# Traced durations in the order generator, and a convolution that reads its products from PSUM

## The chip, the cores and the metric

The kernel runs on one core of one Trainium2 chip. A core has five engines that each run their own queue of instructions strictly in order: TensorE (PE, matrix multiplies, with its weight loads shown as PEld), VectorE (DVE), ScalarE (ACT), GpSimd (POOL) and SyncE (SP, which here only issues DMA transfers). They wait for each other through semaphores. Matrix products land in PSUM, an accumulator memory that the kernel uses as eight banks of 128 x 512 float32; everything else on the chip lies in SBUF. The metric is the device time of one execution in microseconds; lower is better.

## The reference, cut to what matters

Two layers over 2048 frames of width 1024, float32. Each layer normalises the frames, scales and shifts them by a conditioning vector, mixes along time, and adds the result back.

```python
def causal_dwconv(x, w):                       # w has 4 taps per channel
    xp = jnp.pad(x, ((0, 0), (k - 1, 0), (0, 0)))
    out = xp[:, 0:s] * w[0]
    for j in range(1, k):
        out = out + xp[:, j:j + s] * w[j]

def rglru_block(h, in_w, conv_w, conv_b, gate_w, gate_b, lam, out_w):       # layer 1
    proj = h @ in_w                            # 1024 -> 2048
    xb, zg = proj[..., :D_RNN], proj[..., D_RNN:]
    xb = causal_dwconv(xb, conv_w) + conv_b
    pre = einsum(xb, gate_w) + gate_b          # 8 blocks of 128, two gates
    r_t, i_t = sigmoid(pre)
    log_a = -8 * r_t * softplus(-lam)
    h_t = exp(log_a) * h_{t-1} + sqrt(1 - exp(2 log_a)) * (i_t * xb)
    return (h * silu(zg)) @ out_w
```

Layer 2 is a gated DeltaNet: a projection 1024 -> 4 x 1024 (q, k, v, z) plus 16 columns, the same 4-tap convolution on q, k and v, a chunked delta rule over 8 heads of 128 channels, a gated norm and an output projection. A last norm ends it.

## The kernel before

**Precision.** Products are made of float32 data split in a high and a low half, so each product of two 1024-deep operands is 8 x 3 matmuls of 128 x 128 weights against 512 columns (`products`, L661 to L668): 24 matmuls, called a job here.

**The order.** Nothing is scheduled at run time. `Weave` (L64 to L135) is a small simulation that runs while the program is built. Every piece of the computation is a Python generator (a thread) that yields what it needs next: an engine with a duration in us (`yield "dve", STT`), a slot of a buffer ring, an event, or a DMA. `run` always lets the thread go next that can start earliest by these durations, and on equal times the one with the lower priority number. The instructions are emitted in that order, so the durations written in the generators decide the order in each engine's queue. They decide nothing else: on the chip an instruction starts when its queue reaches it and its semaphores are met. A third value in a `yield` replaces the default lag (0.2 to 0.3 us) after which a result counts as seen by another engine. The names for the common durations stand at L241: `STT`, `EV`, `CP`, `TR`, `MM`, `M4` for a tap, a VectorE pass over 512 columns, a ScalarE copy, a transpose, a product matmul and a small matmul of 128 columns.

**Layer 1** (two halves of 1024 frames, each in two groups of 512; profile time to about 516 us). For each of 8 channel blocks there is an x panel and a z panel of weights; each makes two jobs, one for each group of frames. `project_thread` runs the jobs one after another at priority 9, so that its products fill whatever TensorE time the other threads leave. A job takes a slot of the PSUM ring `mm` (two banks), for x and for z alike. The other rings of PSUM are `tp`, `c` and `d`, two banks each; `d` is used in layer 1 only for transposes at the start.

- An x job goes to `conv1_thread`: `extend` has POOL copy the last four frames of the group before (L721 or L725), ACT copy the product from PSUM to the SBUF tile `xe` (L727), after which the bank is free, and POOL save the new last four frames (L730). Then POOL makes the first tap with the bias (`xf`, L741), and DVE adds the other three taps one by one in `taps` (L715), each reading `xe` and `xf` and writing `xf`.
- A z job goes to `z1_thread`: ACT makes a tanh from PSUM (L750), DVE combines it with the product in PSUM (L752), after which the bank is free.
- `gates_thread` splits `xf` in halves (`xh` by ACT, L765; `xl` by DVE, L768), runs two times three gate matmuls (`pg`, L774), two tanh, an exp and a square root on ACT, six passes of DVE with the scan over time (L805), two passes of POOL (L792, L812), and stores the result.

Beside this the weights of each panel are split (ACT L643, POOL L649), the second half of the frames is normalised, transposed and split, and the conditioning of layer 2 is computed (L412 on DVE).

**Out1** (about 516 to 696 us) is the output projection of layer 1: 32 jobs.

**Layer 2** (about 696 to 1784 us): 128 jobs, a convolution with `extend`, POOL L958 and the same `taps`, and for each of 8 heads and 16 blocks of 128 frames the delta rule. `recurrence_thread` is a chain of short steps: two products with the state (`pp`, L1369), `zt` on DVE (L1378), `py` on PE (L1386), `yt` on ACT (L1392), `pS` on PE (L1398), the new state on DVE (L1411). The jobs of the projection are put between these steps by the generator. **Out2** (from about 1784 us): 16 blocks of 128 frames.

Of the kernel before, what the change touches and what calls it, by code (L numbers as in the profile page):

```python
# [8 lines left out]
F32 = mybir.dt.float32  # L9
F32R = mybir.dt.float32r  # L10
# [55 lines left out]
class Weave:  # L66
# [8 lines left out]
    LAG = {"pe": 0.2, "act": 0.3, "dve": 0.3, "pool": 0.2}  # L75

    def __init__(self):
        self.free = dict.fromkeys(("pe", "act", "dve", "pool", "sp", "dma"), 0.0)
        self.threads = []
        self.now = 0.0  # L80
# [19 lines left out]
    def start(self, th):  # L100
# [8 lines left out]
        return max(th.t, self.free.get(w[0], 0.0))  # L109

    def run(self):
        while self.threads:
# [26 lines left out]
def trunk_kernel(ctx, tc, x, c, ada_w, ada_b, ada_c, norm_c, final_g, w1, cw1, cb1, gate_w, gate_b, lam, ow1,  # L139
# [21 lines left out]
    def flat(ap):  # L161
# [13 lines left out]

    middle = cp.tile([P, P], F32, name="middle")
    pool.tensor_copy(out=middle, in_=upper)
    pool.tensor_scalar(middle[0:64, :], middle[0:64, :], -1.0, 0.0, ALU.add, ALU.add)
# [15 lines left out]
    carry1 = cp.tile([P, KT, 4], F32, name="carry1")  # L194
# [6 lines left out]
            "ss": ("xp", 4), "rs": ("xp", 4)}  # L201
    tags |= {f"tf{n}": ("l1", 1) for n in range(6)}
    tags |= {t: ("ps", 2) for t in ("mm", "tp", "c", "d")}
    tags |= {t: ("l1", n) for t, n in {"xe1": 2, "xf1": 2, "tg": 4, "th": 2, "tz": 2, "gw": 1, "gh": 1, "gl": 1, "ada": 1, "ng": 1}.items()}
    tags |= {"yf": ("o1", 1), "yh": ("o1", 2), "yl": ("o1", 2), "xr": ("o1", 2), "g1": ("o1", 1)}
    tags |= {t: ("l2", n) for t, n in {
        "xe": 2, "xf": 2, "kt": KTN, "qt": QTN, "vt": 1, "ec": 3, "gr": 1, "ac": 4, "atn": 4, "kd": 4, "vn": 4,
# [4 lines left out]
    for t in ("xe", "xf", "vt", "ec", "gr", "ab", "gin", "gg", "spe", "spd"):  # L212
        tags[t] = ("l2a", tags[t][1])
# [27 lines left out]
    STT, EV, CP, TR, MM, M4 = 0.665, 0.605, 0.48, 0.109, 0.2163, 0.218  # L241
# [203 lines left out]
    def scale_thread(xt, done):  # L445
# [12 lines left out]
        yield "dve", STT  # L458
# [97 lines left out]
    def split_thread(layer, pt, release_, hh, hl, k, done, tag):  # L556
# [3 lines left out]
        yield "act", 0.665  # L560
# [7 lines left out]
        else:  # L568
            yield "dve", 0.33
# [4 lines left out]
        else:  # L574
            yield "dve", EV
# [35 lines left out]
    def panels_thread():  # L611
        yield ev("adaissue", 2)
        ahead = []
        for name, panels, _ in plans:
            for m, p in enumerate(panels):
# [31 lines left out]
                else:  # L647
                    yield "pool", 2.3
# [21 lines left out]
    def job(name, jobs, n):  # L670
# [8 lines left out]
        mtok = yield slots["mm"]  # L679
        pt = ps.tile([P, TC], F32, tag="mm", name="mm")  # L680
# [4 lines left out]
        if layer == 1:  # L685
            w.spawn((conv1_thread if kind == "x" else z1_thread)(u, m, i, pt, mtok), 2, 0.2)
# [30 lines left out]
    def extend(xe, pt, mtok, carry, key, g):  # L717
# [4 lines left out]
        else:  # L722
            yield ev("carry", key, g - 1)
            yield "pool", 0.14
# [4 lines left out]
        yield "pool", 0.14, 0.0  # L729
# [3 lines left out]
    def conv1_thread(u, n, i, pt, mtok):  # L733
        etok = yield slots["xe1"]
        xe = tile_([P, TC + 4], "xe1", "xe1")
# [1007 lines left out]
```

## Time and profile before

| what | value |
|---|---|
| median of 3 runs | 1986.4 us (1982.22 to 1989.81) |
| the profiled execution's own time | 1980.38 us |
| its span, first to last instruction | 1978.6 us |
| mean granted TensorE clock | 0.985 |
| busy: PE, DVE, ACT, POOL | 93%, 75%, 53%, 37% |
| HBM traffic over the span | 162 GB/s |

The span is what the trace resolves; the own time has 1.8 us around it. "Busy" counts the time in which at least one instruction of an engine runs. The matmuls of TensorE overlap each other, so a matmul row shows about 400 ns while matmuls start about 227 ns apart.

### The profile page before, as it was taken

The page shows a single profiled execution, that of the slowest core. Times are in us where ns is not written, and L with a number is a line of the kernel's source. Part 1 is how long each engine was busy: PE and PEld are TensorE (multiplying, and loading weights), DVE is VectorE, ACT ScalarE, POOL GpSimd, SP SyncE. Part 2 cuts the span into 40 slices and gives each one's busy share as a digit, 9 for nine tenths or more (in the row PEclk, how much of TensorE's full clock was granted, in tenths as well). Part 3 has the DMA queues.
Part 4 walks back from the last instruction along what each step waited for, and adds up shares of the span by engine and source line. Part 5 has one row for each costly group of instructions (what it writes and reads, how often), then busy time and mean ns, then how long its engine had stood idle before and what let it go on. Part 6 is the DMA issues. An engine that isn't in the chain of part 4 may idle for free.

```text
span 1978.6 us, 31398 instructions
## 1 busy us (share of the span) xinstructions
PE 1846.2 (93%) x10286; PEld 1500.3 (76%) x10286; DVE 1475.7 (75%) x3171; ACT 1046.7 (53%) x2555; POOL 724.1 (37%) x1215
## 2 busy tenths in 40 slices
PE   6998889999998998898989999999999999999998
PEld 3776667787787777777777778777888888878887
DVE  6788798887644567778977898567778778877654
ACT  3655567666411236465555555555656566654321
POOL 4555664444200135345344544333333334311101
PEclk9999999999999999999999999999999999999999
DMA  8355655654578724547764457455465555577751
GB/s 334 103 157 158 223 168 169 200 178 153 175 198 210 225 74 140 145 114 176 189 161 130 119 125 191 128 147 147 119 152 147 131 133 140 149 219 221 225 186 64
DMA packets 511724, 322.77 MB, mean 163 GB/s; under 512 B 371268, under 2 KB 439236, under 8 KB 511560
## 3 DMA queue, kind: packets, MB, share of 16 engines
q1 hardware_dynamic: 511560, 320.77, 57.4%
q8 instruction: 81, 1.33, 0.3%
q14 instruction: 83, 0.68, 0.1%
HBM read 219.93 MB, written 100.73 MB: 162 GB/s over the span
## 4 chain that ended last, share of the span: by engine, by line
PE 46%; DVE 21%; DMA 10%; issue 6%; ACT 6%; POOL 5%; SPq 5%; DVEq 0%; POOLq 0%; ACTq 0%
PE mm L667 21%; PE mmo L667 12%; DVE xf L715 6%; DMA raw<-in_w 2%; DVE ttmp L1249 2%; DVE tblk L1252 2%; PE pg L774 1%; DMA xt<-x_d 1%; SPq L1187 1%; SPq L512 1%; DVE acc L412 1%; PE pp L1369 1%; PE pS L1398 1%; PE pkk L1129 1%; PE pS L1399 1%
## 5 line engine op out<-in xcount | busy, mean ns | idle before, releaser
L715 DVE SCALAR_TENSOR_TENSOR xf<-xe,cw_s,xf 128x512 f32<-128x512 f32 x384 | 331.4, 866 | 46.7 <-POOL xf L958 24.1
L649 POOL TENSOR_TENSOR wlo<-raw,whi 128x1024 fp32r<-128x1024 f32 x48 | 120.6, 2512 | 99.7 <-ACT whi L643 81.2
L1249 DVE TENSOR_TENSOR ttmp<-blk,tblk 128x60 f32<-128x60 f32 (+24 forms) x496 | 118.3, 238 | 24.9 <-DMA blk<-blk_d 11.5
L643 ACT CAST whi<-raw 128x1024 fp32r<-128x1024 f32 x96 | 100.4, 1045 | 64.5 <-DMA raw<-in_w 54.7
L1252 DVE TENSOR_TENSOR tblk<-tblk,ttmp 128x60 f32<-128x60 f32 (+24 forms) x496 | 122.3, 247 | 10.0 <-POOL tblk L1243 0.2
L730 POOL COPY carry<-xe 128x4 f32<-128x4 f32 x128 | 40.3, 315 | 239.2 <-ACT xe L727 237.1
L727 ACT COPY xe<-mm 128x512 f32<-128x512 f32 x128 | 73.9, 578 | 74.0 <-PE mm L667 73.0
L667 PE MATMUL mm<-hh_('in2', 0)_5201,whi 128*128 128x512 f32 x256 | 105.0, 410 | 4.1 <-ACT xe L727 4.1
L667 PE MATMUL mmo<-oh,yh 128*128 128x512 f32 x256 | 101.1, 395 | 7.8 <-DVE xr L922 7.2
L667 PE MATMUL mm<-hh_('in2', 1)_12203,whi 128*128 128x512 f32 x256 | 105.2, 411 | 2.8 <-ACT xe L727 2.8
L667 PE MATMUL mm<-hh_('in2', 0)_5424,whi 128*128 128x512 f32 x256 | 103.7, 405 | 2.1 <-ACT xe L727 1.5
L667 PE MATMUL mm<-hh_('in2', 0)_5201,wlo 128*128 128x512 f32 x256 | 105.3, 411 | 0.0
L667 PE MATMUL mm<-hl_('in2', 0)_5425,whi 128*128 128x512 f32 x256 | 104.9, 410 | 0.0
L667 PE MATMUL mm<-hl_('in2', 0)_5202,whi 128*128 128x512 f32 x256 | 104.6, 409 | 0.0
L667 PE MATMUL mm<-hh_('in2', 1)_12379,wlo 128*128 128x512 f32 x256 | 104.4, 408 | 0.0
L667 PE MATMUL mm<-hh_('in2', 1)_12203,wlo 128*128 128x512 f32 x256 | 104.4, 408 | 0.0
L667 PE MATMUL mm<-hh_('in2', 0)_5424,wlo 128*128 128x512 f32 x256 | 104.0, 406 | 0.0
L667 PE MATMUL mm<-hl_('in2', 1)_12204,whi 128*128 128x512 f32 x256 | 103.8, 405 | 0.0
L667 PE MATMUL mm<-hl_('in2', 1)_12380,whi 128*128 128x512 f32 x256 | 103.2, 403 | 0.0
L667 PE MATMUL mm<-hh_('in2', 1)_12379,whi 128*128 128x512 f32 x256 | 103.1, 403 | 0.0
L667 PE MATMUL mmo<-oh,oh 128*128 128x512 f32 (+1 forms) x264 | 102.0, 386 | 0.2 <-DVE tz L986 0.2
L667 PE MATMUL mmo<-ol,oh 128*128 128x512 f32 (+1 forms) x264 | 102.1, 387 | 0.0
(324 smaller groups left out, 5698.7 us busy)
## 6 DMA issues: line engine op xcount, KB each, us to landing
raw<-in_w SPq DMA_DIRECT2D x96, 512.0 KB, 4.2
araw<-in_ada_w SPq DMA_DIRECT2D x32, 512.0 KB, 4.4
xt<-x_d SPq DMA_DIRECT2D x32, 512.0 KB, 4.5
xt_d<-xb SPq DMA_DIRECT2D x192, 64.0 KB, 2.6
xk<-xt_d SPq DMA_DIRECT2D x24, 512.0 KB, 5.5
xt<-in_x SPq DMA_DIRECT2D x16, 512.0 KB, 4.9
ada<-in_ada_w SPq DMA_DIRECT2D x16, 512.0 KB, 9.1
y_d<-tz SPq DMA_DIRECT2D x32, 256.0 KB, 3.1
```

The source lines that it names most:

```text
L412: dve.scalar_tensor_tensor(acc, raw[:, k, :], ck, acc, ALU.mult, ALU.add)
L512: sp.dma_start(out=dst[c_], in_=tb[32 * c_:32 * c_ + 32])
L643: act.copy(hi, raw)
L649: pool.tensor_tensor(lo, raw, f(hi), ALU.subtract)
L667: pe.matmul(pt, lhsT=lhs[a][:, k, :], rhs=rhs[b][:, k, :], start=(k == 0 and n == 0), stop=(k == KT - 1 and n == 2))
L715: dve.scalar_tensor_tensor(xf, xe[:, 1 + j:1 + j + TC], wc[:, j:j + 1], xf, ALU.mult, ALU.add)
L727: act.copy(xe[:, 4:4 + TC], pt)
L730: pool.tensor_copy(out=carry, in_=xe[:, TC:TC + 4])
L774: pe.matmul(pg, lhsT=a[:, g, :], rhs=b, start=(q == 0), stop=(q == 2))
L1129: pe.matmul(pkk[:, b, :], lhsT=kc, rhs=kc, start=True, stop=True)
L1249: dve.tensor_tensor(tmp, blk[:, j, j + 1:32].unsqueeze(2).to_broadcast([P, r, c_]), t[:, j, 0:c_].unsqueeze(1).to_broadcast([P, r, c_]), A ...
L1252: dve.tensor_tensor(t[:, j + 1:32, 0:c_], t[:, j + 1:32, 0:c_], tmp, ALU.subtract)
```

## The change

Three things change together.

1. **The durations.** The names at L241 and some thirty further durations of the generators are replaced by others. `STT` 0.665 to 0.78, `EV` 0.605 to 0.61, `CP` 0.48 to 0.49, `TR` 0.109 to 0.112, `MM` 0.2163 to 0.2275, `M4` 0.218 to 0.23. Other examples: the weight split on POOL 2.3 to 2.45, the scan 0.665 to 1.41, POOL's last pass of the gates 1.23 to 1.42, its four-column copies 0.14 to 0.27, the passes of the gates on DVE 0.605 to between 0.69 and 0.85, scaling a block of `ec` 0.14 to 0.27, the four groups of tiny matmuls of `levels_thread` 0.38, 0.88, 0.4 and 0.9 to 1.1, 1.1, 1.0 and 1.1. `Weave` also gets a kind of matmul `mm` for the 512-column products, which costs 0.087 more when the matmul before it was a small one.
2. **The convolution of layer 1 reads PSUM.** The copy to `xe` and POOL's three instructions for an x job go. ACT makes the last tap with the bias from PSUM into `xf`, columns 3 to 511, and copies the first three and last three columns of the product to a small tile `edge1`. DVE adds the other three taps, reading the product in PSUM and `xf` in SBUF, and the bank is then free. The first three columns of `xf` come from `edge1` by a multiply, a reduction and an addition of the bias, on tiny shapes.
3. **Four banks.** z jobs of layer 1 take a bank of the ring `d`, x jobs stay on `mm`.

Besides, `xh` gets a ring of its own (it shared one with `xe`), and the constant `middle` is made when layer 2 begins instead of at the start. What is computed stays the same. The core of the diff:

```diff
+    SWITCH = 0.087
+    ENGINE = {"mm": "pe"}
...
-                self.free[w[0]] = t + w[1]
-                th.t = t + w[1] + (w[2] if len(w) > 2 else self.LAG[w[0]])
+                dur = w[1]
+                if w[0] in ("pe", "mm"):
+
+                    if w[0] == "mm" and self.small:
+                        dur += self.SWITCH
+                    self.small = w[0] == "pe"
+                e = self.ENGINE.get(w[0], w[0])
+                self.free[e] = t + dur
+                th.t = t + dur + (w[2] if len(w) > 2 else self.LAG[e])
...
-    STT, EV, CP, TR, MM, M4 = 0.665, 0.605, 0.48, 0.109, 0.2163, 0.218
+    STT, EV, CP, TR, MM, M4 = 0.78, 0.61, 0.49, 0.112, 0.2275, 0.23
...
-                yield "pe", dur, 0.0
+                yield "mm", dur, 0.0
...
-        mtok = yield slots["mm"]
-        pt = ps.tile([P, TC], F32, tag="mm", name="mm")
+
+        bank = "d" if layer == 1 and kind == "z" else "mm"
+        mtok = yield slots[bank]
+        pt = ps.tile([P, TC], F32, tag=bank, name="mm")
...
+    def convolve(xf, pt, mtok, wc, bias, edge, key, g, bank):
+
+
+        yield "act", 0.66 if bias is not None else 0.57, 0.0
+        if bias is None:
+            act.activation(xf[:, 3:TC], pt[:, 3:TC], AF.Copy, scale=wc[:, 3:4])
+        else:
+            act.activation(xf[:, 3:TC], pt[:, 3:TC], AF.Identity, bias=bias, scale=wc[:, 3:4])
+        yield "act", 0.18, 0.1
+
+        if g < S // TC - 1:
+            act.copy(edge[:, 6 * g + 3:6 * g + 9].rearrange("p (a b) -> p a b", b=3), window(pt[:, 0:3], (TC - 3, 2), (1, 3)))
+        else:
+            act.copy(edge[:, 6 * g + 3:6 * g + 6], pt[:, 0:3])
+        w.set(ev("edge", key, g))
+        for j in range(3):
+            yield "dve", STT, 0.13 if j < 2 else 0.05
+            dve.scalar_tensor_tensor(xf[:, 3:TC], pt[:, j:j + TC - 3], wc[:, j:j + 1], xf[:, 3:TC], ALU.mult, ALU.add)
+        put(bank, mtok)
+        if g > 0:
+            yield ev("edge", key, g - 1)
+        etok = yield slots["ed"]
+        yield "dve", 0.09, 0.1
+        pr = tile_([P, 3, 4], "ed", "ed")
+        dve.tensor_tensor(pr, window(edge[:, 6 * g:6 * g + 3], (1, 3), (1, 4)), wc.unsqueeze(1).to_broadcast([P, 3, 4]),
+                          ALU.mult)
+        yield "dve", 0.09, 0.1
+        dve.tensor_reduce(out=xf[:, 0:3], in_=pr, axis=mybir.AxisListType.X, op=ALU.add)
+        if bias is not None:
+            yield "dve", 0.14, 0.1
+            dve.tensor_scalar(xf[:, 0:3], xf[:, 0:3], bias, None, ALU.add)
+        put("ed", etok)
...
     def conv1_thread(u, n, i, pt, mtok, bank):
-        etok = yield slots["xe1"]
-        xe = tile_([P, TC + 4], "xe1", "xe1")
         yield ev("columns")
-        yield from extend(xe, pt, mtok, carry1[:, n, :], ("x", n), u * NTC + i)
         ftok = yield slots["xf1"]
-        yield "pool", 0.76
         xf = tile_([P, TC], "xf1", "xf1")
-        pool.tensor_scalar(xf, xe[:, 1:1 + TC], cw1_s[:, n, 0:1], cb1_s[:, n:n + 1], ALU.mult, ALU.add)
-        yield from taps(xe, xf, cw1_s[:, n, :])
-        put("xe1", etok)
+        yield from convolve(xf, pt, mtok, cw1_s[:, n, :], cb1_s[:, n:n + 1], edge1[:, n, :], ("x", n), u * NTC + i, bank)
```

More of the change, by code (lines that the diff above doesn't have):

```diff
@@ L75 @@
     LAG = {"pe": 0.2, "act": 0.3, "dve": 0.3, "pool": 0.2}
+    SWITCH = 0.087
+    ENGINE = {"mm": "pe"}
     def __init__(self):
         self.free = dict.fromkeys(("pe", "act", "dve", "pool", "sp", "dma"), 0.0)
+        self.small = True
         self.threads = []
@@ L210, in trunk_kernel @@
         "gs": 2, "eg": 2}.items()}
-    for t in ("xe", "xf", "vt", "ec", "gr", "ab", "gin", "gg", "spe", "spd"):
+    for t in ("xe", "xf", "vt", "ec", "gr", "middle", "ab", "gin", "gg", "spe", "spd"):
         tags[t] = ("l2a", tags[t][1])
@@ L559, in split_thread @@
         ttok = yield slots[tag]
-        yield "act", 0.665
+        yield "act", 0.71
         h = tile_([P, TC], tag, "h")
@@ L685, in job @@
         if layer == 1:
-            w.spawn((conv1_thread if kind == "x" else z1_thread)(u, m, i, pt, mtok), 2, 0.2)
+            w.spawn((conv1_thread if kind == "x" else z1_thread)(u, m, i, pt, mtok, bank), 2, 0.2)
         elif kind == "z":
@@ L744, in conv1_thread, with z1_thread @@
         w.set(ev("xf", u, n, i), (xf, ftok))
-    def z1_thread(u, n, i, pt, mtok):
+    def z1_thread(u, n, i, pt, mtok, bank):
         ztok = yield slots["tz"]
@@ L752, in z1_thread @@
         dve.scalar_tensor_tensor(tz, tz, 1.0, pt, ALU.add, ALU.mult)
-        put("mm", mtok)
+        put(bank, mtok)
         w.set(ev("tz", u, n, i), (tz, ztok))
@@ L775, in gates_thread @@
             w.spawn(gate_thread(u, n, i, g, pg, ctok), 3)
-        put("xe1", etok)
+        put("xh", etok)
         put("xr", ltok)
@@ L945, in phase1_end_thread @@
         enter("l2", "l2a")
+        middle = tile_([P, P], "middle", "middle")
+        pool.tensor_copy(out=middle, in_=upper)
+        pool.tensor_scalar(middle[0:64, :], middle[0:64, :], -1.0, 0.0, ALU.add, ALU.add)
+        w.set(ev("middle"), middle)
         w.set(ev("l2"))
@@ L1045, in decay_thread @@
         yield "pe", 1.1
+        middle = yield ev("middle")
         pgc = ps.tile([P, 3, NB * NH], F32, tag="tp", name="pgc")
@@ L1449, in outputs_thread @@
         for b in range(TB):
-            yield "act", 0.255, 0.0 if b < TB - 1 else 0.27
+            yield "act", 0.295, 0.0 if b < TB - 1 else 0.27
             act.activation(oo[:, b, :], oo[:, b, :], AF.Copy, scale=ro[:, b:b + 1])
```

81 lines of the change are left out of this document (41 added, 40 removed).

## The prediction

> **What bounds the kernel now.** I read the table of stages first, then the waits of TensorE by stage, then one stall in order of time, then the rows of the instructions that the change touches. The boundaries of the stages are where the kind of work changes; 310 splits layer 1 where the normalising and splitting of its second half has ended.
>
> ```profile
> core 0: us, PE busy (x) PEld busy (x) DVE busy (x) ACT busy (x) POOL busy (x), PEclk, DMA share, GB/s
> 0.00:50.00 50.00, 30.52 (x103) 18.03 (x104) 32.83 (x75) 18.87 (x32) 21.44 (x34) 0.94 0.87 331
> 50.00:310.00 260.00, 228.91 (x945) 179.65 (x945) 219.43 (x259) 158.76 (x223) 154.85 (x151) 0.95 0.52 158
> 310.00:500.00 190.00, 184.47 (x809) 148.77 (x808) 157.67 (x198) 130.84 (x171) 80.12 (x93) 1.00 0.56 180
> 500.00:700.00 200.00, 189.25 (x815) 152.82 (x814) 107.59 (x143) 50.21 (x63) 29.44 (x35) 0.99 0.69 201
> 700.00:1400.00 700.00, 647.89 (x4102) 529.11 (x4100) 546.04 (x1464) 393.51 (x1195) 292.21 (x544) 0.99 0.56 143
> 1400.00:1790.00 390.00, 383.46 (x2649) 319.80 (x2648) 304.70 (x896) 241.25 (x749) 124.56 (x304) 1.00 0.59 153
> 1790.00:1979.00 189.00, 181.67 (x878) 152.11 (x875) 107.48 (x141) 53.30 (x126) 21.51 (x55) 0.99 0.54 166
> ```
>
> TensorE is the bound: 1846 of 1979 us busy, and from 1400 on almost without a hole. What a change can win is its idle time, length minus busy: 19.5, 31.1, 5.5, 10.8, 52.1, 6.5 and 7.3 us. In 50 to 310 it idles 12.0% of the time, in 310 to 500, with the same kind of job, 2.9%; DVE is about as busy in both (84% and 83%), but POOL has 60% in the one and 42% in the other. The granted clock is 0.95 against 1.00 as well, so the early stage loses twice. As all later work of TensorE follows in line, a microsecond won here should come off the end, as long as nothing else is late at the hand-over.
>
> Who ends the idle time, in 50 to 310 and then in 310 to 500:
>
> ```profile
> PE pg L774 <- DVE xl L768: 20.9, 9, 5.2
> PE pg L774 <- ACT xh L765: 1.2, 3, 0.6
> ```
> ```profile
> PE pg L774 <- DVE xl L768: 0.8, 3, 0.3
> ```
>
> So 22.1 of the 31.1 us (71%) are nine to twelve stalls of the gate matmuls, which wait for the halves of `xf`, the convolution's result. One of them, in order of time, by engine (POOL, DVE, PE; start, length):
>
> ```profile
> 122.36 1.27 POOL L812 TENSOR_TENSOR tz<-tz,tg 128x512 f32<-128x512 f32 x1
> 123.59 2.79 POOL L649 TENSOR_TENSOR wlo<-raw,whi 128x1024 fp32r<-128x1024 f32 x1
> ```
> ```profile
> 122.30 1.87 DVE L715 SCALAR_TENSOR_TENSOR xf<-xe,cw_s,xf 128x512 f32<-128x512 f32 x1 [0.51 <-POOL xf L741]
> 124.10 0.70 DVE L506 STREAM_TRANSPOSE xb<-xt 128x512 f32<-128x512 f32 x1
> 124.73 2.21 DVE L715 SCALAR_TENSOR_TENSOR xf<-xe,cw_s,xf 128x512 f32<-128x512 f32 x1
> 126.86 0.68 DVE L768 TENSOR_TENSOR xl<-xf,xh 128x512 fp32r<-128x512 f32 x1
> ```
> ```profile
> 121.94 0.39 PE L667 MATMUL mm<-hl_('in1', 0)_481,whi 128*128 128x512 f32 x1
> 122.17 0.39 PE L667 MATMUL mm<-hh_('in1', 0)_480,wlo 128*128 128x512 f32 x1
> 122.58 0.49 PE L774 MATMUL pg<-xh,gh 128*128 128x512 f32 x1
> 127.59 0.80 PE L774 MATMUL pg<-xl,gh 128*128 128x512 f32 x1 [4.52 <-DVE xl L768]
> 128.19 0.63 PE L774 MATMUL pg<-xh,gl 128*128 128x512 f32 x1
> 128.61 0.63 PE L667 MATMUL mm<-hh_('in1', 0)_480,whi 128*128 128x512 f32 x1
> ```
>
> TensorE stands 4.52 us for `xl`, which is queued on DVE behind two taps that take 1.87 and 2.21 us while POOL runs. After it matmuls start 0.42 us apart instead of 0.23: the clock was lowered, and that is the second loss. Now what a tap costs, and what it could cost from PSUM (shortest, median, longest ns of all; then the means in 50 to 310):
>
> ```profile
> L715 DVE SCALAR_TENSOR_TENSOR xf<-xe,cw_s,xf x384: 702/747/2935, 58.4 to 1737.2; 128x512 f32<-128x512 f32 x192
> ```
> ```profile
> L752 DVE SCALAR_TENSOR_TENSOR tz<-tz,mm x32: 655/680/690, 61.4 to 507.1; 128x512 f32<-128x512 f32 x32
> ```
> ```profile
> L715 DVE SCALAR_TENSOR_TENSOR xf<-xe,cw_s,xf 128x512 f32<-128x512 f32 x51 | 58.3, 1142 | 11.0 <-POOL xf L741 10.8
> ```
>
> The same operation with one input in PSUM (`mm`) never took more than 690 ns, with POOL just as busy around it; with both inputs in SBUF it takes 1142 in this stage.
>
> **The change part by part.** *Taps on DVE, 50 to 310.* 51 taps x (1.142 - 0.680) = 23.6 us less busy, and the 10.8 us in which DVE waits for POOL's first tap go too. What is late next there is ACT's first tap, which starts right at the product's end. *Added on DVE*, for each of 17 x jobs: a multiply, a reduction and an addition on 3 columns. The nearest rows:
>
> ```profile
> L271 DVE TENSOR_TENSOR cond<-acol,ada_s 128x4 f32<-128x4 f32 x2 | 0.3, 153 | 0.0
> L261 DVE TENSOR_SCALAR sp<-sp 128x8 f32<-128x8 f32 x7 | 1.2, 172 | 0.2
> ```
>
> 17 x (0.153 + 0.153 + 0.172) = 8.1 us. The multiply has both inputs in SBUF, and may be held as the old taps are: 1142 - 747 = 395 ns more on the mean, 17 x 0.395 = 6.7 us as the other end; I take none, since the early rows were not held. DVE's queue gets 23.6 + 10.8 - 8.1 = 26.3 us shorter (19.6 at the other end), about as much as TensorE idles there.
>
> Here two pages of the Trainium skill bear. "SBUF — State Buffer", section "Who interferes with whom", says that a VectorE instruction with two SBUF inputs and a GpSimd one that reads SBUF exclude each other for the whole instruction, and that one with at most one SBUF input does not contend; the taps agree (2935 against at most 690 ns), but it speaks against the new multiply, and by it the 19.6 would be the likelier figure. "VectorE: DVE Perf Modes", section "Rules for kernel authors", advises copying PSUM to SBUF first when many operations follow, which is what the change undoes; its errata section puts 62 cycles at 0.96 GHz on a PSUM source, so an estimate of 51 x 65 ns = 3.3 us that the sum would lose. The row says otherwise: 680 from PSUM against a median of 747.
>
> *POOL, 50 to 310:*
>
> ```profile
> L741 POOL TENSOR_SCALAR xf<-xe,cw_s,cb_s 128x512 f32<-128x512 f32 x17 | 22.3, 1310 | 0.8 <-DVE tg L794 0.6
> L730 POOL COPY carry<-xe 128x4 f32<-128x4 f32 x17 | 8.0, 470 | 6.6 <-ACT xe L727 6.6
> L725 POOL COPY xe<-carry 128x4 f32<-128x4 f32 x10 | 4.7, 469 | 1.5 <-DVE xf L715 1.5
> ```
>
> 35 us less, from 154.9 to 120: 46% of the stage, near the 42% of 310 to 500, where the same jobs hardly stall. *ACT* gets a tap of the kind of `tg` and a tiny copy for its copy to `xe`:
>
> ```profile
> L824 ACT ACTIVATE tg<-pg,gb_s 128x512 f32<-128x512 f32 x62 | 41.7, 686 | 22.4 <-PE pg L774 22.2
> L727 ACT COPY xe<-mm 128x512 f32<-128x512 f32 x31 | 18.1, 584 | 44.8 <-PE mm L667 44.6
> L311 ACT ACTIVATE c_th<-c_col 128x8 f32<-128x8 f32 x1 | 0.2, 208 | 0.5 <-DMA c_col<-in_c 0.5
> ```
>
> 17 x (0.686 + 0.208 - 0.584) = 5.3 us on 158.8: 63% instead of 61%, hidden by ACT's own idle time; without that cover it is 5.3 us. Queued behind the tiny copy is only ACT's next work, and the taps don't wait for it.
>
> *The banks.* An x bank is held for 0.7 + 0.2 + 3 x 0.68, about 3 us, plus the time in DVE's queue, where ACT freed it in 0.6. With z on `d`, the same bank comes up again after three more jobs of 24 x 0.227 = 5.4 us, so 16.3 us later. I cost it at nothing; were the hold as long as 17.3 us, each x job would stall 1 us, 32 in all. `middle` is two small POOL instructions at another place, nothing. DMA: none is added or moved past a queue by itself; the order of issues shifts with the plan.
>
> *Layer 1, sum.* If 50 to 310 came to the 2.9% of 310 to 500, it would idle 7.6 us, a gain of 23.5; and the clock back at 1.00 is worth 0.05 x 260 = 13. Together 36.5, the upper end; the lower is 0, if the new order stalls elsewhere. 71% of the idle time hangs on `xl` and `xh`, so I take 0.71 x 36.5 = 26, and 1 for the 0.8 of the next stage: **27 us**.
>
> *The durations, elsewhere.* They move no work, only places in the queues. In 50 to 310 they belong to the 27: the old plan has a tap at 0.665 against 1.142 and so places the gate matmuls too early. In layer 2 the taps stay in SBUF; who ends TensorE's idle time in 700 to 1400, and the taps there:
>
> ```profile
> PE mm L667 <- ACT xe L727: 8.4, 5, 2.8
> PE pS L1398 <- ACT yt L1392: 6.9, 9, 1.6
> PE pp L1369 <- DVE state L1411: 5.8, 4, 1.9
> ```
> ```profile
> L715 DVE SCALAR_TENSOR_TENSOR xf<-xe,cw_s,xf 128x512 f32<-128x512 f32 x180 | 151.8, 849 | 20.0 <-POOL xf L958 16.4 <-POOL xe L721 2.2
> ```
>
> A plan nearer to 849 ns (0.78 for 0.665) should place waits better: up to half of 52.1 + 6.5, so 29 us. Against it, the new plan leaves less cover in the recurrence (rival 2): up to 44 us worse. The ends lie on both sides, no row shows the new order, and I take 0. Stage 500 to 700 and the start keep their work: 0.
>
> The profiled execution took 1980.38 us (span 1978.6). 1980.4 - 27 = 1953.4. The median of the runs is 1986.4 / 1980.38 = 1.003 times that execution, so 1953.4 x 1.003 = **1959 us**.
>
> **The rivals.** *1. Nothing on the path.* The stalls move from `xl` to another late operand (`acc` of the conditioning, the weight split), or what layer 1 wins is given back in layer 2 by the new places. For it: 29% of the idle time has other causes, and 52 us of stalls in layer 2 are spread over many waits, which any new order shuffles. Against: nine stalls with one cause. Time: 1986. That the change doesn't do what it says is part of this: PSUM taps as slow as before would leave DVE its 23.6 us.
>
> *2. Slower, through the recurrence of layer 2.* Between the steps of a block the plan fills TensorE's waits with product matmuls. By the old numbers a block waits (0.2 + 0.27 + 0.3) + (0.2 + 0.16 + 0.3) + (0.2 + 0.27 + 0.3) = 2.20 us, room for 2.20 / 0.2163 = 10.2 products; by the new ones 2.23 - 3 x 0.087, divided by 0.2275, is 8.7. So 1.5 products less, 0.34 us, in 16 blocks x 8 heads: 44 us, if every wait is already as long as its cover. Less the 27: 17 slower, 1997.4 x 1.003 = 2003. It turns the sign from 27 / 44, so 61% of the blocks uncovered, and passes 0.5% from about 84%. For it: `pS`, `pp` and `mm` stall already in 700 to 1400. Against: 1400 to 1790 idles only 1.7%, so there the cover has room, and later planned DVE times put products back.
>
> *3. Layer 2 gains too.* The 29 us above on top of the 27: 1924.4 x 1.003 = 1930. For it: DVE's waits dominate and its durations were the ones most wrong. Against: rival 2.
>
> **How the numbers follow.** About 0.5% is what a measurement of this kernel can tell from no change: 1976 to 1996. Forecast, 1940 to 1976: 0.54. Rival 3, around 1930: 0.14. Rival 1, 1976 to 1996: 0.16. Rival 2, around 2003: 0.16. Faster 0.68, same 0.16, slower 0.16. The range leaves out rival 2 and the outer end of rival 3 and holds the rest: 1920 to 1997.
>
> **What would show it.** Right: taps of layer 1 at 650 to 700 ns with no long ones; DVE's wait for POOL's first tap gone; the wait of `pg` for `xl` from 20.9 us to a few; clock near 0.99 in 50 to 310; out1 starting some 27 us sooner; no waits of products for a bank. Wrong: PSUM taps of 0.85 us or more; a tiny multiply of over 0.5 us; TensorE's idle time in layer 2 well away from 58.6 us, in either direction, which would outweigh the 27.

## The result, and the profile after

The changed kernel takes a median of 2018.87 us (4 runs, 2016.46 to 2022.96), the kernel before, run beside it, 1984.31 us (4 runs, 1978.78 to 1989.81). The ratio is 1.0172, with an interval from 1.015 to 1.0194: **slower by 1.7%**, where a gain of 1.4% was forecast. The profiled execution took 2016.46 us, its span is 2014.7.

First the table of stages of the kernel after, with the same boundaries as before (length; busy time and instructions of PE, PEld, DVE, ACT, POOL; granted clock; DMA share; GB/s):

```profile
50.00:310.00 260.00, 245.57 (x1050) 195.70 (x1051) 230.85 (x328) 165.52 (x250) 111.48 (x101) 0.98 0.59 174
310.00:500.00 190.00, 187.16 (x818) 151.01 (x817) 153.92 (x239) 124.25 (x177) 55.17 (x56) 1.00 0.54 174
...
700.00:1400.00 700.00, 627.86 (x3960) 508.02 (x3959) 535.20 (x1411) 382.36 (x1167) 285.69 (x533) 0.98 0.55 141
1400.00:1790.00 390.00, 367.93 (x2461) 303.27 (x2460) 289.41 (x871) 227.77 (x726) 119.06 (x301) 0.99 0.53 136
```

TensorE's idle time (length minus busy) went from 31.1 to 14.4 us in 50 to 310 and from 5.5 to 2.8 in 310 to 500. It rose from 52.1 to 72.1 in 700 to 1400 and from 6.5 to 22.1 in 1400 to 1790. So layer 1 did what was hoped and layer 2 did the contrary. What each stage won or lost is read from where its work begins. In order of time, the first product of out1 and the first of out2, before and then after:

```profile
504.75 0.39 PE L667 MATMUL mmo<-oh,yh 128*128 128x512 f32 x1
1783.83 0.50 PE L667 MATMUL mmo<-oh,oh 128*128 128x512 f32 x1 [0.22 <-DVE tz L986]
```
```profile
477.14 0.40 PE L674 MATMUL mmo<-oh,yh 128*128 128x512 f32 x1
1820.25 0.40 PE L674 MATMUL mmo<-oh,oh 128*128 128x512 f32 x1
```

Then the first product line of layer 2 by its tile (shortest, median, longest ns; first and last start), before and after:

```profile
L667 PE MATMUL mm<-hh_('in2', 0)_5201,whi x256: 387/393/632, 695.9 to 1237.5; 128*128 128x512 f32 x128
```
```profile
L674 PE MATMUL mm<-hh_('in2', 0)_5233,whi x256: 387/393/795, 673.4 to 1232.2; 128*128 128x512 f32 x128
```

Out1 starts 504.75 - 477.14 = 27.6 us sooner. Layer 2 starts 695.9 - 673.4 = 22.5 us sooner, so out1 gave back 5.1. Layer 2 lasts 1783.83 - 695.9 = 1087.9 us before and 1820.25 - 673.4 = 1146.9 after: **59.0 us lost**. Out2 starts 1820.25 - 1783.83 = 36.4 us later, and the span ends 2014.7 - 1978.6 = 36.1 later, so from there on nothing changed.

Layer 1 by its instructions, from the rows of four lines of the convolution after:

```profile
L762 DVE SCALAR_TENSOR_TENSOR xf<-mm,cw_s,xf x96: 697/739/749, 58.9 to 476.0; 128x509 f32<-128x509 f32 x96
```
```profile
L769 DVE TENSOR_TENSOR ed<-edge,cw_s x32: 121/159/2376, 62.6 to 476.7; 128x12 f32<-128x12 f32 x32
```
```profile
L772 DVE TENSOR_REDUCE xf<-ed x32: 116/154/166, 62.8 to 477.9; 128x3 f32<-128x12 f32 x32
```
```profile
L775 DVE TENSOR_SCALAR xf<-xf,cb_s x32: 178/220/2439, 63.0 to 478.6; 128x3 f32<-128x3 f32 x32
```

A tap from PSUM is never over 749 ns: nothing holds it any more. Two of the three tiny operations are at times held for over 2 us. The waits that remain in 50 to 310, of PE and of DVE (total, times, longest):

```profile
PE pg L813 <- DVE xl L807: 8.9, 10, 1.7
```
```profile
DVE xf L762 <- ACT edge L756: 6.0, 5, 2.0
```

`pg` for `xl` fell from 20.9 to 8.9 us and the longest from 5.2 to 1.7. No product waits for a bank. Now layer 2, each kernel in its own stretch, first the stretch itself, then who ends TensorE's idle time and three of ACT's waits, before and after:

```profile
696.00:1784.00 1088.00, 1029.35 (x6690) 847.56 (x6689) 846.93 (x2354) 630.95 (x1936) 418.11 (x849) 0.99 0.56 145
```
```profile
673.00:1820.00 1147.00, 1050.22 (x6770) 853.29 (x6769) 856.89 (x2362) 633.14 (x1944) 414.56 (x852) 0.98 0.53 139
```
```profile
PE pS L1398 <- ACT yt L1392: 9.1, 12, 1.6
PE mm L667 <- ACT xe L727: 8.4, 5, 2.8
```
```profile
PE pS L1443 <- ACT yt L1437: 27.6, 23, 3.0
...
PE py L1431 <- DVE zt L1423: 9.2, 10, 1.8
```
```profile
ACT whi L643 <- DMA raw<-in_w: 40.4, 27, 5.5
...
ACT junkq L1167 <- DMA pq<-q_d: 17.6, 19, 2.3
ACT vn L1203 <- DMA vn<-v_d: 14.1, 7, 4.0
```
```profile
ACT whi L650 <- DMA raw<-in_w: 51.7, 31, 9.3
ACT vn L1248 <- DMA vn<-v_d: 39.5, 18, 5.9
...
ACT junkq L1212 <- DMA pq<-q_d: 26.2, 23, 4.7
```

DVE, ACT and POOL do the same work in the same time to within 10 us. TensorE idles 96.8 us instead of 58.7, the clock falls from 0.99 to 0.98 (an estimate from two-digit figures: 0.01 x 1088 = 11 us), and the rest of the 59 is busy time, which these records give only to a per cent or two (80 more of them). Added up by the engine that ends them, the idle times that end with ACT grow from 21.0 to 44.7 us, those that end with DVE from 37.0 to 51.2. The state product `pS` waits three times as long for `yt`, a step of ACT. And ACT stands in front of three loads for 117 us instead of 72. These two rows, and the question of which causes which, led the experiments.

### The profile page after: what moved, and what is told of

Same layout as the page of the kernel before. It is cut to its first block, busy times and chain, and to the rows that moved or that the text cites. A ratio compares the mean times of both kernels' runs of the same rounds, so it can differ in the third digit from the quotient of the medians.

```text
span 2014.7 us, 31428 instructions
## 1 busy us (share of the span) xinstructions
PE 1861.1 (92%) x10286; PEld 1499.0 (74%) x10286; DVE 1474.0 (73%) x3267; ACT 1031.4 (51%) x2573; POOL 641.1 (32%) x1120
## 4 chain that ended last, share of the span: by engine, by line
PE 36%; DMA 18%; DVE 17%; ACT 10%; issue 8%; SPq 6%; POOL 4%; DVEq 0%; POOLq 0%; ACTq 0%
PE mm L674 17%; PE mmo L674 11%; DMA raw<-in_w 3%; DMA pq<-q_d 3%; DMA q_d<-tb 2%; DVE xf L724 2%; DVE tblk L1297 2%; DMA x_d<-xr 1%; SPq L519 1%; ACT junkq L1212 1%; DVE ttmp L1294 1%; ACT junk L1150 1%; SPq L1232 1%; PE pg L813 1%; DMA oraw<-in_ow 1%
## 5 line engine op out<-in xcount | busy, mean ns | idle before, releaser
L674 PE MATMUL mm<-hh_('in2', 0)_5457,whi 128*128 128x512 f32 x256 | 105.9, 414 | 2.1 <-DVE tz L1030 1.4
L674 PE MATMUL mm<-hh_('in2', 1)_12216,whi 128*128 128x512 f32 x256 | 105.5, 412 | 1.9 <-ACT xe L736 1.9
L674 PE MATMUL mm<-hh_('in2', 0)_5457,wlo 128*128 128x512 f32 x256 | 105.4, 412 | 0.0
L674 PE MATMUL mm<-hl_('in2', 0)_5458,whi 128*128 128x512 f32 x256 | 105.1, 411 | 0.0
L674 PE MATMUL mm<-hl_('in2', 1)_12217,whi 128*128 128x512 f32 x256 | 105.1, 411 | 0.0
L674 PE MATMUL mm<-hh_('in2', 1)_12216,wlo 128*128 128x512 f32 x256 | 105.1, 410 | 0.0
L674 PE MATMUL mm<-hh_('in2', 1)_12445,wlo 128*128 128x512 f32 x256 | 104.7, 409 | 0.0
L674 PE MATMUL mm<-hh_('in2', 1)_12445,whi 128*128 128x512 f32 x256 | 104.7, 409 | 0.0
L674 PE MATMUL mm<-hl_('in2', 1)_12446,whi 128*128 128x512 f32 x256 | 104.6, 409 | 0.0
L674 PE MATMUL mm<-hh_('in2', 0)_5233,wlo 128*128 128x512 f32 x256 | 104.1, 407 | 0.0
```

The costliest lines, as they stand in the source:

```text
L674: pe.matmul(pt, lhsT=lhs[a][:, k, :], rhs=rhs[b][:, k, :], start=(k == 0 and n == 0), stop=(k == KT - 1 and n == 2))
```

## The experiments

Each run was timed against the kernel before on the same chip. The table gives what all of them showed; "L2" is the time from the first product of layer 2 to the first of out2, "loads" the sum of ACT's waits for `raw`, `vn` and `pq` in it, "idle" TensorE's idle time in it, all from the one profiled execution, so a few us in these are not a difference. The ratio is taken over all executions of a kernel.

| kernel | ratio, interval | out1 starts | L2 | loads | idle |
|---|---|---|---|---|---|
| before | 1 | 504.8 | 1088 | 72 | 59 |
| after | 1.0172, 1.015 to 1.0194 | 477.1 | 1147 | 117 | 97 |
| e1 taps and banks only | 0.9975, 0.9951 to 0.9999 | 494.2 | 1100 | 81 | 66 |
| e2 durations only | 1.0244, 1.0211 to 1.0276 | 496.8 | 1154 | 118 | 96 |
| e3 layer 2: PE old | 1.0067, 1.0042 to 1.0092 | 479.2 | 1114 | 82 | 69 |
| e4 layer 2: vector old | 1.0228, 1.0212 to 1.0243 | 479.2 | 1158 | 102 | 87 |
| e5 longer lag of yt | 1.023, 1.0204 to 1.0257 | 481.4 | 1149 | 118 | 98 |
| e6 all lags longer | 1.016, 1.0136 to 1.0184 | 479.4 | 1140 | 145 | 89 |
| e7 layer 2: all old | 0.9948, 0.9926 to 0.997 | 479.3 | 1097 | 73 | 61 |
| e8 null, on before | 1.0009, 0.9991 to 1.0028 | 505.0 | 1091 | 73 | 59 |
| e9 layer 2: lead 2.2 | 0.9941, 0.9911 to 0.9971 | 479.5 | 1089 | 59 | 56 |
| e10 no switch cost | 1.0061, 1.0037 to 1.0084 | 478.5 | 1123 | 109 | 70 |
| e11 matmuls old | 1.0106, 1.0083 to 1.013 | 479.4 | 1117 | 96 | 74 |
| e12 levels old | 1.0088, 1.006 to 1.0115 | 481.8 | 1126 | 119 | 80 |
| e13 e7 with lead 2.2 | 0.991, 0.9887 to 0.9934 | 479.4 | 1089 | 54 | 54 |
| e14 layer 2: lead 3.5 | 0.9944, 0.9927 to 0.996 | 479.1 | 1091 | 53 | 60 |
| e15 lead for vn, pq only | 1.0155, 1.0119 to 1.0192 | 479.1 | 1143 | 88 | 90 |
| e16 lead for panels only | 1.024, 1.0215 to 1.0264 | 480.2 | 1157 | 96 | 93 |

**Which half of the change.** e1 keeps the convolution from PSUM and the four banks and puts every old duration back; e2 is the kernel before with the new durations alone.

```diff
-    STT, EV, CP, TR, MM, M4 = 0.78, 0.61, 0.49, 0.112, 0.2275, 0.23
+    STT, EV, CP, TR, MM, M4 = 0.665, 0.605, 0.48, 0.109, 0.2163, 0.218
...
-                yield "mm", dur, 0.0
+                yield "pe", dur, 0.0
```

> The taps from PSUM and the four banks alone, with every duration of the order generator as before. Theory A (the new PE durations take product matmuls out of the gaps of the recurrence) and theory B (the new durations of DVE, ACT and POOL move the heads' work): the loss of layer 2 goes, and layer 1 keeps a part of its gain, so 1955 to 1975 us, and the wait of pS for yt is near the 9 us of before. Theory C (the loss comes from the taps, the banks or middle themselves): over 2000 us.

> The durations alone, with the convolution of layer 1 and its two banks as before. Theories A and B: layer 2 loses about as it did with the whole change and layer 1 gains at most half, so 2015 to 2045 us, and the wait of pS for yt stays near 28 us. Theory C: about 1985 us.

The loss belongs to the durations: e2 alone is 2.4% slower and its layer 2 is as long as after's. The taps win 504.8 - 494.2 = 10.6 us in layer 1 and the durations alone 8.0; only together they win 27.6. So e1, at a median of 1980.7 us, lies above the 1955 to 1975 expected: it has less of layer 1's gain, and its layer 2 is 12 us longer than before.

**Which durations.** e3 takes the old durations of PE's work in layer 2, e4 most of those of DVE, ACT and POOL there (not those of the weight split, of `EV` and `CP`, and of splitting the frames).

```diff
-        yield from products(pt, (hi, lo), h, (lambda k: ev("split", (name, i), k)))
+        yield from products(pt, (hi, lo), h, (lambda k: ev("split", (name, i), k)), MM if layer == 1 else 0.2163)
...
+        w.SWITCH = 0.0
...
-        yield "pe", 1.1
+        yield "pe", 0.38
```
```diff
-            yield "dve", STT, 0.13 if j < 3 else 0.27
+            yield "dve", 0.665, 0.13 if j < 3 else 0.27
...
-                yield "act", 0.19
+                yield "act", 0.16
```

> The whole change, but from layer 2 on the PE durations of before: products at 0.2163 without the 0.087 after a small matmul, small matmuls at 0.218, the tiny groups of the levels at 0.38, 0.88, 0.4 and 0.9. Theory A: four products again between py and pS, the wait of pS for yt at 8 to 14 us, 1955 to 1985 us. Theory B: 2005 to 2020 us and the wait stays near 28 us.

> The whole change, but in layer 2 the durations of DVE, ACT and POOL of before (taps 0.665, four-column copies 0.14, ec 0.14, yt 0.16, the 32-column steps 0.065 and so on), with the new PE durations. Theory A: three products between py and pS in most blocks, the wait stays at 20 to 35 us, 2000 to 2025 us. Theory B: 1955 to 1985 us.

In the profiled execution PE's old durations bring back 33 of the 59 us and bring `pS`'s wait for `yt` from 27.6 to 6.4. That execution is the fastest of six; by the medians e3 recovers 17.6 us (2001.25 against 2018.87). Of the 26 us by which its layer 2 is still longer than before, 10 are idle time; the rest is busy time, at a clock of 0.96. The old vector durations with PE's new ones bring nothing (2032.6 us). Neither time lies in a range that was expected for it.

**Is it the cover?** The count of products between the last `py` and the first `pS` of a block, in the trace, is most often 4 before (79 of 128 blocks) and 3 after (69). If that missing cover is the cause, giving it back must help. e5 lengthens the lag after which `yt` counts as seen from the default 0.3 to 0.42, e6 does it for `zt`, `yt` and the state.

```diff
-                yield "act", 0.19
+                yield "act", 0.19, 0.42
```
```diff
-                    yield "dve", 0.27
+                    yield "dve", 0.27, 0.55
...
-                yield "act", 0.19
+                yield "act", 0.19, 0.6
...
-                yield "dve", 0.27
+                yield "dve", 0.27, 0.55
```

> The whole change with one number more: after the ACT step yt of the recurrence the generator counts the result as seen 0.42 us later instead of 0.3. By the durations of the changed kernel that makes room for four products between py and pS where there were three. Theory A (the cover of that gap): the wait of pS for yt falls from 27.9 to 8 to 14 us and the time by 12 to 22 us, to 1997 to 2007 us. If the cover of this gap isn't the cause: 2014 to 2025 us.

> The whole change with longer lags after all three vector steps of the recurrence (zt and the state 0.55, yt 0.6 instead of 0.3), so that four to five products fit in each gap. Theory A: the waits of pS, py and pp for these steps fall from about 47 us to under 15, and the time to 1975 to 1998 us, unless the chain of a head, each step of which is then planned longer, becomes the bound. Rival: the loss lies in other waits (kt, qt, the levels), which stay, 2005 to 2020 us.

PE's waits in e5 (its layer 2), then in e6 (the whole run):

```profile
PE py L1431 <- DVE zt L1423: 18.0, 14, 2.4
PE pS L1443 <- ACT yt L1437: 14.5, 15, 2.8
PE mm L674 <- ACT xe L736: 13.9, 6, 5.5
PE pp L1414 <- DVE state L1456: 11.9, 10, 2.0
```
```profile
PE pS L1443 <- ACT yt L1437: 27.2, 24, 3.3
```

In e5 four products lie in the gap in 83 blocks and the wait halves, but `zt`, `xe` and the state are waited for longer and the time, 2032.7 us, is no better, above both ranges expected. In e6 (2017.8 us, in the rival's range) four or five products lie there in 99 blocks, and `yt` is still 27.2 us late: it is not late by a fraction of a product, it is late because ACT itself stands. Adding up the waits of ACT that reach into the 2 us before each such late `yt`, its queue stood 14.0 us in front of `vn`, 6.7 of `pq` and 6.7 of `raw`; in the trace of after it is 7.5, 3.4 and 6.4. ACT runs its queue in order, so `yt`, queued behind an instruction that waits for a load, waits as well. This theory, **ACT stands for loads that the plan puts too early**, replaced the one of the cover.

**Two controls.** e7 keeps layer 1 as changed and goes back to all old durations where layer 2 begins. e8 is the kernel before with one duration changed by 2 ns, which reshuffles its order in many places.

```diff
+        nonlocal STT, EV, CP, TR, MM, M4
+        STT, EV, CP, TR, MM, M4 = 0.665, 0.605, 0.48, 0.109, 0.2163, 0.218
+        w.SWITCH, w.late = 0.0, True
```
```diff
-    STT, EV, CP, TR, MM, M4 = 0.665, 0.605, 0.48, 0.109, 0.2163, 0.218
+    STT, EV, CP, TR, MM, M4 = 0.667, 0.605, 0.48, 0.109, 0.2163, 0.218
```

> The whole change in layer 1 and out1, and from the start of layer 2 on every duration of the generator as before. If the loss is that of layer 2's new durations and nothing else: layer 1 keeps its 27 us, layer 2 takes 1088 to 1100 us as it did before and with the old durations throughout, 1955 to 1972 us. If any new order of layer 2 costs, whatever its durations: 1980 to 2005 us.

> The kernel before with the duration of a tap 0.667 instead of 0.665: no reason for a gain or a loss, but the order of the instructions changes in many places. It measures what an order of the same quality gives by chance. If the order before is an ordinary one: 1975 to 1995 us. If it is a lucky one, as a rival for part of the loss: 1995 to 2015 us.

e8 costs nothing, so the order before was no stroke of luck that this reshuffle would spoil. e7 keeps layer 1's gain and loses 9 us of it in layer 2; its 1976.0 us lie just above the 1955 to 1972 expected.

**The loads' lead.** The generator counts a transfer as seen `SEEN` = 0.92 us after its planned end; nothing else in it says how late data come. These lines set it:

```python
self.free["dma"] = max(t + 1.13, self.free["dma"]) + w[1] / 360e3
th.t = self.free["dma"] + self.SEEN if len(w) < 3 or w[2] else t + 0.48
```

For a panel of 512 KB, with nothing ahead of it, that is 1.13 + 1.46 + 0.92 = 3.5 us from the issue, and the page of after says 4.2 us to landing at the median:

```profile
raw<-in_w SPq DMA_DIRECT2D x96, 512.0 KB, 4.2
```

For `vn` and `pq`, of 256 KB, the same sum is 1.13 + 0.73 + 0.92 = 2.78 us, and layer 2 of after shows 2.9 for both (one is shown):

```profile
vn<-v_d SPq DMA_DIRECT2D x32, 256.0 KB, 2.9
```

So a transfer itself is priced 0.7 us too short for a panel and 0.1 for the two others. Over ACT's 31 waits for panels and 41 for the others that is 31 x 0.7 + 41 x 0.12 = 27 of the 117 us, an estimate from the medians; counted wait by wait in the trace it is 23.5. The rest is loads that are issued late for ACT's turn, not loads that take long. One place where that happens is SP's own queue, which is in order too: before the load of `pq` (L1161, then L1206) it stands for the store that this load reads back. Before and after, layer 2:

```profile
SPq L1161 <- DMA q_d<-tb: 27.6, 27, 3.9
```
```profile
SPq L1206 <- DMA q_d<-tb: 40.3, 32, 3.9
```

`SEEN` stands for both: how late data count as there, and how late what waits for a store is issued.

The old plan priced a product matmul at 0.2163 us where they start some 0.227 apart, and two of the four groups of `levels_thread` at 0.38 and 0.4 where the new plan has 1.1 and 1.0, so on the chip the planned intervals were stretched, and the loads had that slack too. The new plan prices PE nearer to the trace and leaves the loads as they were. This is an argument; e9 tests what would follow from it: the whole change, with `SEEN` at 2.2 from the beginning of layer 2. e10 to e12 each take one part of PE's new durations back there: the cost of a switch, that of the matmuls themselves, and the four groups of `levels_thread` (the first is shown).

```diff
         enter("l2", "l2a")
+        w.SEEN = 2.2
```
```diff
         enter("l2", "l2a")
+        w.SWITCH = 0.0
```
```diff
-                    yield "mm", MM, 0.0
+                    yield "mm", 0.2163, 0.0
```
```diff
-        yield "pe", 1.1
+        yield "pe", 0.38
```

> The whole change, but from layer 2 on the generator counts a DMA's data as seen 2.2 us after the planned end of its transfer instead of 0.92. Theory D (with the longer PE durations the plan lets ACT meet loads of vn, pq and panels too early, ACT stands in its queue, and the recurrence's yt behind it is late): ACT's waits for these loads fall from 117 us to under 85 and the time to 1980 to 2000 us. If the early meeting is a symptom only: 2010 to 2030 us.

> The whole change without the 0.087 us after a small matmul from layer 2 on; the other PE durations new. If this surcharge is what makes the order bad (it falls on three gaps of every recurrence block, 33 us in the plan): 1985 to 2003 us. If it is the length of the products or the levels: 2012 to 2030 us.

> The whole change with products at 0.2163 and small matmuls at 0.218 in layer 2, the surcharge and the levels new. If the length of the products is the cause (3072 of them, 34 us in the plan, beside an unchanged model of the DMA): 1985 to 2003 us. If not: 2012 to 2030 us.

> The whole change with the four groups of tiny matmuls of the levels at 0.38, 0.88, 0.4 and 0.9 again. They are 16 heads x 1.74 us in the plan, 28 us in all. If they are the cause: 1985 to 2003 us; if not: 2012 to 2030 us.

e9's layer 2, PE's wait there and ACT's two longest for loads:

```profile
673.00:1762.00 1089.00, 1032.97 (x6656) 844.67 (x6655) 855.23 (x2348) 629.55 (x1934) 415.30 (x848) 0.99 0.56 144
```
```profile
PE pS L1444 <- ACT yt L1438: 5.4, 7, 1.9
```
```profile
ACT whi L650 <- DMA raw<-in_w: 29.0, 21, 3.1
...
ACT vn L1249 <- DMA vn<-v_d: 18.4, 11, 6.1
```

One constant, and no duration of the change undone: layer 2 is back at 1089 us, the median at 1978.04 against 2018.87 (40.8 us less, and just under the 1980 to 2000 expected), the clock at 0.99. The profiled execution is the fastest of five, and its out2, which runs with the longer lead too, takes 1965.6 - 1762.1 = 203.5 us where after's takes 194.4; so the median gains less than layer 2 does. `pS` waits 5.4 us, although most blocks (77 of 128) still have only three products in the gap. Of TensorE's idle time in layer 2, what ends with ACT falls from 44.7 to 11.9 us, what ends with DVE from 51.2 to 42.5: four fifths of the idle time that goes were waits for ACT. So the cover was not what was missing, and the planned lead of the transfers carries the loss. e10, e11 and e12 each recover a part (18, 9 and 12 us of the median), so no single price did it; e3, with all three prices old, recovers no more than e10 does alone, so the parts don't add up. Of their ranges only e10's was met.

**How far, and which transfers.** e13 is e7 with `SEEN` at 2.2, e14 is e9 with 3.5; e15 gives 1.28 us more only behind the loads of `vn` and `pq`, e16 only to the panels `raw` and their low halves.

```diff
-        w.SWITCH, w.late = 0.0, True
+        w.SWITCH, w.late, w.SEEN = 0.0, True, 2.2
```
```diff
-        w.SEEN = 2.2
+        w.SEEN = 3.5
```
```diff
+        yield "none", 1.28
```
```diff
-    def arrive_thread(event, value=True):
-        yield "none", w.free["dma"] + w.SEEN - w.now
+    def arrive_thread(event, value=True, more=0.0):
+        yield "none", w.free["dma"] + w.SEEN + more - w.now
...
-        w.spawn(arrive_thread(ev("raw", name, p)), 0)
+        w.spawn(arrive_thread(ev("raw", name, p), more=1.28 if layer == 2 else 0.0), 0)
```

> As the run with every old duration in layer 2 (1976 us), with the DMA's data counted as seen after 2.2 us there instead of 0.92. If it is a matter of proportion between PE and DMA in the plan, the old durations were near balance: ACT's waits for loads fall by at most 20 us from 73 and the time is 1962 to 1985 us. If loads met too early cost by themselves, whatever the other durations: a gain of over 20 us, under 1956 us.

> The whole change with data seen 3.5 us after the planned end of a transfer in layer 2. Theory D with the real latency near the 2.2 already tried: ACT's waits for loads stay under 60 us, no further gain, 1970 to 1995 us, as each head's chain is now planned too long. If the plan is still too early at 2.2: 1950 to 1968 us.

> The whole change with 1.28 us more after the loads of vn and pq alone (the same lead as 2.2 gives them), all other loads as in the change. If ACT's standing before values and queries is what makes yt late: their 66 us of waits fall to 30 to 40, the wait of pS for yt from 28 to 8 to 15 us, 1985 to 2003 us. If it is the panels: 2010 to 2025 us.

> The whole change with 1.28 us more after the loads of layer 2's weight panels alone (raw, and the low halves in the second half), all other loads as in the change. If ACT's standing before a panel is what costs: its 52 us of waits fall to 25 to 35 and the time is 1985 to 2003 us. If it is values and queries: 2010 to 2025 us.

ACT's waits and PE's in layer 2 of e15:

```profile
ACT whi L650 <- DMA raw<-in_w: 62.9, 38, 4.4
...
ACT vn L1250 <- DMA vn<-v_d: 14.3, 9, 3.8
ACT junkq L1213 <- DMA pq<-q_d: 10.5, 8, 3.1
```
```profile
PE pS L1445 <- ACT yt L1439: 13.7, 19, 2.1
```

More lead than 2.2 brings nothing more (e14, 1976.7 us). With the old durations the longer lead is worth 6 us of the median (1975.97 to 1969.96, with intervals that overlap), with the new ones 40.8: so it mends what the new durations broke. Leads for some loads alone take those waits away (e15: `vn` and `pq` from 65.7 to 24.8 us, `pS`'s wait halved; e16: `raw` from 51.7 to 31.5) without any gain in time: e15's 2018.8 us lie in the range for the other cause, e16's 2034.7 above both. In e15 ACT's wait for `raw` rises instead, from 51.7 to 62.9, and TensorE's idle time that ends with ACT falls to 28.8 us while that with DVE rises to 59.0: the standing moves. The four new orders that leave the lead of some or all loads as it was and keep PE's durations, e5, e6, e15 and e16, lie at 2018 to 2035 us, e9 and e14 at 1977 to 1978, so a lucky order is an unlikely rival for the 41 us. **e13, at 1969.96 us and a ratio of 0.991, has the lowest median of this study, 0.9% below before;** its interval overlaps those of e9 and e14.

## Why the prediction was wrong

**Layer 1: 27 us predicted, 27.6 measured**, at the start of out1. The stall that it named is the one that went: `pg` for `xl` from 20.9 to 8.9 us, DVE's wait for POOL's first tap gone, the clock from 0.95 to 0.98. The sum that gave the 27 came out nearly term by term: idle time in 50 to 310, 0.71 x 23.5 = 16.7 forecast and 31.1 - 14.4 = 16.7 measured; the clock, 0.71 x 13 = 9.2 forecast and 0.03 x 260 = 7.8 measured, to two digits; the next stage 1 and 2.7. What was said to bring this about, DVE's queue, was less right.
- Taps at 0.739 us, not 0.680. At the mean of 0.738, 51 x (1.142 - 0.738) = 20.6 us instead of 23.6.
- The tiny operations at 0.321 + 0.152 + 0.380 = 0.85 us for a job on the mean of 50 to 500, not 0.48. For 17 jobs that is 14.5 us, about the 8.1 with the other end of 6.7 added (14.8). The added end had been laid on the multiply alone; the bias addition was held as well.

```profile
L775 DVE TENSOR_SCALAR xf<-xf,cb_s 128x3 f32<-128x3 f32 x32 | 12.2, 380 | 0.2
...
L769 DVE TENSOR_TENSOR ed<-edge,cw_s 128x12 f32<-128x12 f32 x32 | 10.3, 321 | 0.0
```

- "What is late next" was ACT's first tap, as said, for 6.0 us. "The taps don't wait for it", said of the tiny copy, was wrong: every wait of a first DVE tap for ACT ends with that copy, not with ACT's tap. It mostly costs under 0.1 us, as here, where ACT's tap ends at 309.62, its copy at 309.68, and DVE starts at 309.71:

```profile
308.85 0.77 ACT L752 ACTIVATE xf<-mm,cb_s,cw_s 128x509 f32<-128x509 f32 x1
309.51 0.17 ACT L756 COPY edge<-mm 128x6 f32<-128x6 f32 x1
```
```profile
309.71 0.75 DVE L762 SCALAR_TENSOR_TENSOR xf<-mm,cw_s,xf 128x509 f32<-128x509 f32 x1 [1.26 <-ACT edge L756]
```

- DVE's queue so gets 20.6 + 10.8 - 14.5 - 6.0 = 10.9 us shorter, not 26.3. This does not explain the gain. In e1, with the old durations, the tiny operations took 0.155 + 0.157 + 0.223 = 0.54 us a job in 50 to 310 and ACT's tap was late for 3.5 us, so DVE's queue got about 20.7 + 10.8 - 9.1 - 3.5 = 18.9 us shorter, more than with the whole change. Yet out1 started only 10.6 us sooner, and `pg` still waited for `xl`:

```profile
PE pg L813 <- DVE xl L807: 14.7, 8, 5.5
```

So the shorter queue alone gives well under half, and the remaining 17 us needed the new durations, which alone give 8.0. That they do so by placing the gate matmuls and their operands nearer to where they come is the reading that fits; no run isolates it. The prediction counted the durations into the 27 but worked nothing out for them, so that the total was met is in part luck.

The banks cost nothing, as costed. Out1 gave 5.1 us back, where "Stage 500 to 700" was put at 0; why is not known.

**The step that failed** is "*The durations, elsewhere*": "They move no work, only places in the queues", costed at 0 with ends at 29 us of gain and 44 of loss. They cost 59 us in layer 2, more than the outer end; e2 alone shows it without the taps, and e7 takes 50 of the 59 back. What the term left out is the lead of the transfers against the new prices: e9 changes that alone and takes the loss away. The sign hung on this term, and its two ends had been set against each other as if they balanced. One of the signs that the prediction named for being wrong is the one that came: TensorE's idle time in layer 2 went from 58.7 to 96.8 us.

**Rival 2** named the right stage, the right sign and the row that grew most (`pS` for `yt`), and gave 2003 us. But its mechanism, fewer products as cover, is refuted: e5 and e6 put the cover back without gain, e9 gains without it. Its "against", that 1400 to 1790 idled only 1.7% and so had room, fell too: that stretch of time idles 22.1 us now. The reading that fits e9 and e13, argued and not shown, is that TensorE's small idle time there rested on loads that came in time only because the plan was too fast for the chip; the view of stages could not show that. The rows of before held the hint: ACT's 72 us of waits for `raw`, `pq` and `vn`, with `yt` in the same queue. The prediction did not read them: it followed PE's waits one step back, to `yt`, and not what stood ahead of `yt` in ACT's queue.

**What is shown and what stays open.** Shown: the new durations make the loss, and 1.28 us more planned lead for all transfers of layer 2 takes layer 2 back to 1089 us and the median down by 41. PE's durations alone carry 18 of the 43 us that e7 recovers; the rest goes only when the vector engines' go too. ACT's standing for loads goes along with the loss (117 us after, 59 in e9), and so does TensorE's idle time behind ACT (44.7 and 11.9), but loads and time do not move in step: e10 and e12 recover time at 109 and 119 us, e16 loses at 96. `SEEN` also delays what waits for stores, `blk`, `tt`, `ec` and the return of buffers, none of which was tried alone. Which transfers carry the 41 us, and whether the lead works by what a transfer takes or by when it is issued, stays open.

## What to carry to other kernels

In an order that is planned ahead, the prices of one resource are right only relative to the others: bringing the engines' durations up to the trace while the transfers kept their old lead turned 27 us won into a loss of 1.7%, and 1.28 us more lead gave 41 us back. So bring transfers and engines up together, and judge each stage by where its work starts and ends, since one stage's gain can hide in another's loss. Before costing a change of order at zero, read the in-order queues for instructions that wait for loads ahead of steps of the critical chain, however idle their engine looks.

## What the hardware showed unexpectedly

An addition of a bias to 128 x 3 elements, with one tensor input, took 220 ns at the median and 2439 at the longest, and a multiply of 128 x 12 elements 159 and 2376, while the reduction between them never went over 166. Of the three, those two are also what the section "Who interferes with whom" of the page "SBUF — State Buffer" in the Trainium skill counts as able to contend with GpSimd for the shared port, and the reduction is what it excludes; the rows agree. The prediction gave the rule without its exception for the modes that use both ports, in which this page of the Trainium skill counts the bias addition's kind. The trace shows too that a tiny shape is no protection: the longest bias addition starts with an instruction of POOL and ends with it (150.69 + 2.40 = 153.09 and 150.68 + 2.44 = 153.12), and the longest multiply ends the same way, at 182.86 where POOL's ends at 182.83.

```profile
150.69 2.40 POOL L656 TENSOR_TENSOR wlo<-raw,whi 128x1024 fp32r<-128x1024 f32 x1 [3.21 <-ACT whi L650]
```
```profile
150.68 2.44 DVE L775 TENSOR_SCALAR xf<-xf,cb_s 128x3 f32<-128x3 f32 x1
```

The tap from PSUM at 739 ns was 9% slower than the other operation of the same kind from PSUM (680), for three columns fewer; what makes the difference was not tried.
